# Products with the high and low halves side by side, and a moved gate conditioning, in a two-layer hybrid block

## The chip, the core and the metric

The kernel runs on one core of one Trainium2 chip, as one launch. The metric is the device time of an execution in microseconds (us), the median over runs. The profile is one execution, taken by the hardware profiler.

## What is computed

Two residual layers act on 256 latent tokens `x`, with 256 context tokens `ctx` beside them; the model width is 2048. Layer 0 is windowed attention with 16 heads and a sink, and it updates both token sets; layer 1 is latent attention (MLA), whose output is wanted for `x` alone.

```python
cond = silu(c); cond_ctx = silu(c_ctx)
for i in range(2):
    shift, scale, gate = split(cond @ ada_w[i] + ada_b[i], 3)     # and *_c from cond_ctx
    h  = rmsnorm(x, norm_g[i]) * (1 + scale) + shift
    hc = rmsnorm(ctx, norm_g[i]) * (1 + scale_c) + shift_c
    o, oc = swa_mixer(h, hc, ...) if i == 0 else mla_mixer(h, hc, ...)
    x = x + gate * o
    if i == 0: ctx = ctx + gate_c * oc
return x

def mixer(h, hc):                      # the outline of both
    q, k, v, g = split(h @ w_in)       # MLA: through two low-rank latents
    o = softmax(q @ k.T * scale + mask) @ v
    return (o * silu(g)) @ w_out
```

`gate` is the third section of the conditioning, `cond @ ada_w[i][:, 4096:]`; it is called the gate conditioning here, and `silu(g)` the output gate.

## The kernel before

**Precision.** Every float32 operand of a large product is split in two: `hi`, rounded to the format float32r, and `lo`, the rest (`split`: ScalarE copies, VectorE subtracts). `mm3` makes one product of three: high by high, high by low, low by high. Weights arrive as `raw` tiles by DMA and become `whi` and `wlo`; activations lie in `h` tiles.

**Stages.** Feature blocks of 128 (`kt`, 16 of them) are the contraction steps. Start: the 16 blocks of `xT` are loaded and squared, the sum of squares gives the norm's factor `rb`, and `ada_first_tasks(0)` makes the first shift and scale; `make_h0(kt)` then makes h. Stage A is the projection to q, k, v of all 512 tokens in five groups of blocks (1, 2, 3, 4 and 6 of them, `GROUPS`); beside a group run as `side` tasks the conditioning products of the next one. Stage B makes the output gates with the attention between. The first output projection (`out0_tasks`) follows: for blocks n below 9 (`XONLY`) first the 256 latent tokens, then blocks 9 to 15 for all 512 tokens at once, then the context half of blocks 0 to 8 (`late`). Layer 1 then has its low-rank projections, queries, keys and output gates (`gate_tasks` with n = 256, 17 of them, since the list holds head 14 twice) with attention between, and the last projection `out1_tasks`, 16 blocks.

In the 256-token products (output gates of layer 1, `out0` for one half, `out1`) the weights stand in the array and 256 tokens stream: three products of 256 columns for a contraction step.

**Gate conditioning.** VectorE makes it (`gate_half`): rows of `ada_w` come as `raw<-adag` tiles of 512 KB, 16 for each half of a layer's contraction, and every tile takes one `scalar_tensor_tensor` with a running sum for each 512 columns and token set. Layer 0's lies in stages A and B, layer 1's two halves (32 tiles) in the first output projection.

**Order.** The program is first noted as a list of operations (`Plan`). `settle` then gives each engine its order by due times (`clock`, `lead`), assumed costs (`cost`) and free buffers; the engines run that order as written. All loads go out of SyncE's (SP) queue, in one order, and `raw` has four buffers.

Of the kernel before, what the change touches and what calls it, by code (L numbers as in the profile page):

```python
# [29 lines left out]
POOL = 0.0  # L30
G0PREP, G0, G0B = 2, {4: (0, None)}, 0.7
# [3 lines left out]
SIDE = [0.85, 0.9, 0.8, 0.95, 1.0]  # L35
# [7 lines left out]
G1, G1CUT = 0.9, 29  # L43
# [93 lines left out]
class ToBe:  # L137


    def __init__(self, pool, shape, dt, tag, bufs, name, space):  # L140
        self.pool, self.shape, self.dt, self.tag = pool, shape, dt, tag
# [19 lines left out]
SWITCH, REACH, TURN, REACHT = 340.0, 20.0, 112.0, 0.0  # L161
DMA_LAT, DMA_RATE = 2000.0, 320.0


class Plan:
# [6 lines left out]
    def pool(self, real, bufs, space="SB"):  # L172
        plan = self

        class Pool:
            def tile(_, shape, dt, tag=None, name=None, bufs_=None, bufs=bufs):
                t = ToBe(real, list(shape), dt, tag, bufs, name, space)
# [126 lines left out]
    def settle(self):  # L304
# [37 lines left out]
        def give(tag):  # L342
            tiles = self.tags[tag]
            while head[tag] < len(tiles) and slots[tag]:
# [4 lines left out]
                s = min(slots[tag], key=lambda s: (s[2] not in (None, t.dt), s[0], s[1]))  # L349
                slots[tag].remove(s)  # L350
                t.slot, t.place = s[:2]
# [10 lines left out]
        while len(out) < len(nodes):  # L362
# [52 lines left out]
            for t in v.tiles:  # L415
                t.done = max(t.done, v.end if e != "PE" else at + v.occ + 120)
                left[id(t)] -= 1
                if not left[id(t)] and t.space != "DRAM":
                    tag = (t.space, t.tag)
                    slots[tag].append((t.done + SEM, t.place, t.dt))  # L420
# [3 lines left out]
    def emit(self):  # L424
# [3 lines left out]
        for v in order:  # L428
            for t in v.tiles:
                if t.real is None:  # L430
# [5 lines left out]
                    had = homes.get((tag, t.place))  # L436
                    if had is None or had[0] != t.dt:
                        had = homes[tag, t.place] = t.dt, t.pool.tile(
                            t.shape if own else [P, size[tag]], t.dt,
                            tag=f"{t.tag}_{t.place}", name=f"{t.name}_{t.place}", bufs=1)  # L440
                    x = had[1]
                    if not own:
                        x = x[:, :int(np.prod(t.shape[1:]))]
# [24 lines left out]
def tile_hybrid_two_layer(ctx: ExitStack, tc: tile.TileContext, a: dict):  # L468
# [4 lines left out]
    hp = plan.pool(ctx.enter_context(tc.tile_pool(name="hp", bufs=32)), 32)  # L473
# [33 lines left out]
    def htile(dt=F32R):  # L507
        return hp.tile([P, 512], dt, tag="h", name=nm("h"))
# [208 lines left out]
    ssq = tpps()  # L717

    def add_squares(sq, first, last):
        for t in range(4):  # L720
            mm(ssq[:, t:t + 1], sq[:, t * P:(t + 1) * P], ones[:, 0:1], first and t == 0, last and t == 3)
# [1165 lines left out]
```

## Time and profile before

| | |
|---|---|
| median of 3 runs | 1250.98 us (1250.64 to 1251.53) |
| profiled execution, its time | 1250.65 us |
| its span, first to last instruction | 1248.9 us |
| TensorE (PE) busy | 1227.3 us, 98% of the span |
| VectorE (DVE) busy | 920.0 us, 74% |
| ScalarE (ACT) busy | 595.8 us, 48% |
| moved by DMA | 249.87 MB, mean 200 GB/s |

The span is 1.75 us shorter than the profiled execution. A busy TensorE is not one at its peak: its matmuls overlap, so the distance between two starts, and not the length of a row, says what one costs.

### The profile page before, as it was taken

The numbers are of one execution on the slowest core, as the hardware profiler recorded it, in microseconds if no ns is written. First come the engines' busy times: TensorE is split into PE (matmuls) and PEld (weight loads), VectorE is DVE, ScalarE is ACT, GpSimd is POOL, SyncE is SP. The second block draws the span as 40 slices with busy tenths as digits, with TensorE's granted clock in tenths as the row PEclk, the third lists the DMA queues.
The fourth block names the chain that finished last, engine by engine and source line by source line (L and its number), as shares of the span: only waits on it lengthen the run. The fifth ranks groups of instructions, "written<-read, shape, count | busy, mean of one in ns | idle before, by whom it ended". The sixth has DMA issues, their size and how long they took to land.

```text
span 1248.9 us, 23671 instructions
## 1 busy us (share of the span) xinstructions
PE 1227.3 (98%) x8828; PEld 1075.7 (86%) x8828; DVE 920.0 (74%) x2255; ACT 595.8 (48%) x1434; POOL 79.1 (6%) x97
## 2 busy tenths in 40 slices
PE   6999999999999999999999999999999999999998
PEld 6788877888888888888899888899999999999998
DVE  3466636698569799977898766886778888878554
ACT  4613212322235445655764223454677777676332
POOL 0000000000001001101000000000111111110000
PEclk9999999999999999999999999999999999999999
DMA  9877677459885656755439967764433333322674
GB/s 324 288 266 251 209 242 240 130 188 334 270 295 199 229 172 230 263 189 180 138 117 289 324 232 246 258 219 118 136 127 111 110 110 110 99 97 85 212 225 138
DMA packets 105524, 249.87 MB, mean 200 GB/s; under 512 B 12352, under 2 KB 26176, under 8 KB 105408
## 3 DMA queue, kind: packets, MB, share of 16 engines
q1 hardware_dynamic: 105408, 248.36, 59.6%
q8 instruction: 69, 1.13, 0.4%
q14 instruction: 47, 0.39, 0.1%
HBM read 239.92 MB, written 8.39 MB: 199 GB/s over the span
## 4 chain that ended last, share of the span: by engine, by line
PE 94%; DVE 3%; DMA 2%; ACT 1%; issue 0%; SPq 0%; ACTq 0%; DVEq 0%
PE mm L236 79%; PE tp L236 8%; PE tp L221 4%; PE s L236 2%; PE s L221 1%; DVE wlo L221 1%; DVE t L221 1%; DMA raw<-adag 0%; DVE acc L221 0%; DMA raw<-wout 0%; DMA k<-ada 0%; DMA h<-xT 0%; ACT whi L221 0%; DVE h L221 0%; ACT t L221 0%
## 5 line engine op out<-in xcount | busy, mean ns | idle before, releaser
L236 PE MATMUL mm<-h,whi 128*128 128x256 f32 (+1 forms) x2368 | 537.4, 319 | 1.9 <-ACT whi L221 1.7
L221 ACT CAST whi<-raw 128x1024 fp32r<-128x1024 f32 (+3 forms) x248 | 243.7, 984 | 374.3 <-PE mm L236 301.8
L236 PEld LDWEIGHTS mm<-h,whi 128*128 128x128 f32 x2368 | 392.0, 191 | 29.3 <-ACT whi L221 2.5
L221 DVE TENSOR_TENSOR wlo<-raw,whi 128x1024 fp32r<-128x1024 f32 (+3 forms) x248 | 282.6, 1141 | 148.3 <-ACT whi L221 141.5
L236 PE MATMUL mm<-h,wlo 128*128 128x256 f32 (+1 forms) x1184 | 378.3, 320 | 3.8 <-DVE wlo L221 3.8
L236 PE MATMUL mm<-whi,h 128*128 128x512 f32 (+2 forms) x1152 | 358.3, 384 | 2.7 <-ACT h L221 2.0
L236 PEld LDWEIGHTS mm<-whi,h 128*128 128x128 f32 x1152 | 213.7, 188 | 44.2 <-issue 4.6
L236 PEld LDWEIGHTS mm<-h,wlo 128*128 128x128 f32 x1184 | 226.1, 191 | 20.2 <-DVE wlo L221 5.7
L236 PE MATMUL mm<-wlo,h 128*128 128x512 f32 (+2 forms) x576 | 220.6, 383 | 0.0
L236 PEld LDWEIGHTS mm<-wlo,h 128*128 128x128 f32 x576 | 108.3, 188 | 18.1 <-issue 0.4
L221 DVE SCALAR_TENSOR_TENSOR t<-raw,acc 128x512 f32<-128x512 f32 x128 | 85.8, 686 | 4.2 <-DMA raw<-adag 2.7
L221 DVE TENSOR_TENSOR acc<-acc,mm 128x512 f32<-128x512 f32 x96 | 63.7, 684 | 26.9 <-PE mm L236 26.6
L236 PE MATMUL mm<-pth,k 128*128 128x256 f32 x256 | 55.4, 289 | 0.0
L221 DVE TENSOR_REDUCE st<-tp 128x1 f32<-128x512 f32 (+1 forms) x76 | 45.9, 605 | 11.2 <-PE tp L236 10.8
L221 POOL TENSOR_TENSOR rr<-rr,mhalf 128x2 f32<-128x2 f32 (+2 forms) x41 | 29.7, 728 | 380.8 <-DVE rr L221 380.0
L236 PE MATMUL tp<-k,q 128*128 128x512 f32 (+1 forms) x189 | 46.4, 361 | 0.0
L221 ACT ACTIVATE cb<-tp,st,rq 128x512 f32<-128x512 f32 (+1 forms) x49 | 33.2, 677 | 27.3 <-DVE st L221 25.9
L221 POOL TENSOR_TENSOR rq<-rq,mhalf 128x2 f32<-128x2 f32 x32 | 27.3, 863 | 297.3 <-DVE rq L221 277.2
L221 POOL TENSOR_TENSOR rk<-rk,mhalf 128x4 f32<-128x4 f32 x20 | 21.9, 1093 | 377.2 <-DVE rk L221 373.8
L221 ACT ACTIVATE t<-acc 128x128 f32<-128x128 f32 (+2 forms) x70 | 26.6, 390 | 40.1 <-DVE acc L221 21.1
L221 ACT CAST pth<-tp 128x512 fp32r<-128x512 f32 x59 | 33.3, 586 | 23.9 <-PE tp L221 23.1
L236 PEld LDWEIGHTS mm<-pth,k 128*128 128x128 f32 x256 | 42.5, 190 | 1.0 <-issue 0.2
(186 smaller groups left out, 1466.5 us busy)
## 6 DMA issues: line engine op xcount, KB each, us to landing
k<-ada SPq DMA_DIRECT2D x128, 256.0 KB, 4.9
raw<-adag SPq DMA_DIRECT2D x64, 512.0 KB, 4.6
acc<-ada SPq DMA_DIRECT2D x128, 256.0 KB, 5.0
raw<-wout SPq DMA_DIRECT2D x47, 512.0 KB, 4.4
raw<-win SPq DMA_DIRECT2D x42, 512.0 KB, 4.6
raw<-mwg SPq DMA_DIRECT2D x34, 512.0 KB, 3.3
raw<-wgate SPq DMA_DIRECT2D x32, 512.0 KB, 5.8
raw<-mwo SPq DMA_DIRECT2D x29, 512.0 KB, 3.8
```

The source lines that it names most:

```text
L221: getattr(real, op)(*r, **k)
L236: getattr(real, op)(*[x.real() if isinstance(x, View) else x for x in args], **{n: x.real() if isinstance(x, View) else x for n, x in kw.i ...
```

## The change

1. **Side by side.** A pair of `h` tiles becomes one tile of 1024 columns (`hpair`). For each 256-token half it holds 256 high and 256 low columns next to each other, and `mmw` takes both in one product of 512 columns with the high weights; a second product of 256 columns adds low weights by high tokens to the first half of the result. The two halves of the result are added afterwards: in `gate_tasks` by an ACT copy and a DVE addition, in `fin_half` and `out1_tasks` by one more DVE operation. It is used for the layer-1 output gates, for `out0` where one half is made, and for `out1` except its last block. `out0` for both halves keeps three products of 512 columns, which now read two pieces of 256 (`both`).
2. **Gate conditioning.** Half of layer 1's (16 tiles) moves from the first output projection to groups 2 and 3 of stage A (`G1PREP`, `G10`).
3. **Start.** Squares are summed by DVE into two tiles instead of by TensorE for every pair of blocks; eight products `ones` by `xT` (`warm`, `WARM`) write a tile that nobody reads; `rms_bcast` works in pieces of 256 columns; `adab` and `normg` load later.
4. **Order.** `settle` lets SP run no further than `BACKLOG` ahead of the DMA it assumes, and hands out pairs of `h` places. This changes the order of loads all over the program.

```diff
-SIDE = [0.85, 0.9, 0.8, 0.95, 1.0]
+G1PREP, G10 = 2, {2: (0, 7), 3: (7, None)}
+WARM = range(6, 14)
+SIDE = [0.85, 0.9, 0.8, 0.9, 1.0]
-G1, G1CUT = 0.9, 29
+G1, G1CUT = 0.9, 17
+BACKLOG = 500.0
...
                 pipe[0] = begin + v.lat / DMA_RATE
                 v.end = pipe[0] + DMA_LAT
+                free[e] = max(free[e], pipe[0] - BACKLOG)
...
+    def hpair():
+        return hp.tile([P, 1024], F32R, tag="h", name=nm("h"), span=2)
...
+    def mmw(ps, lh, ll, pair, first, last):
+
+
+        mm(ps, lh, pair, first, False)
+        mm(ps[:, :256], ll, pair[:, :256], False, last)
...
-        sq = tmp()
-        S.activation(sq, t, AF.Square)
-        if kt % 2 and kt < KT - 1:
-            V.tensor_tensor(even, even, sq, op=ALU.add)
-            add_squares(even, kt == 1, False)
-        elif kt < KT - 2:
-            even = sq
+        if kt < 2:
+            S.activation(ssq[kt], t, AF.Square)
         else:
-            add_squares(sq, False, kt == KT - 1)
-    adab = const("adab", [P, 2, 48])
-    normg = const("normg", [P, 2, KT])
+            sq = tmp()
+            S.activation(sq, t, AF.Square)
+            V.tensor_tensor(ssq[kt % 2], ssq[kt % 2], sq, op=ALU.add)
+        if kt in WARM:
+
+            mm(warm, ones, t, True, True)
+            clock[0] = 0.0
+    with plan.lead(-4.0):
+        adab = const("adab", [P, 2, 48])
+        normg = const("normg", [P, 2, KT])
...
-                    hh, hl = h[kt] if n == NT else h1[0][kt]
-                    mm3(ps[:, :n], wh[:, us], wl[:, us], hh, hl, kt == 0, kt == KT - 1)
+                    if n == NT:
+                        mm3(ps, wh[:, us], wl[:, us], *h[kt], kt == 0, kt == KT - 1)
+                    else:
+                        mmw(ps, wh[:, us], wl[:, us], o0[kt][:, :512], kt == 0, kt == KT - 1)
...
+            if n == NX:
+                g = th[:, NX:]
+                S.copy(g, ps[:, NX:])
+                V.tensor_tensor(g, ps[:, :NX], g, op=ALU.add)
+                ps = g
...
+        if gi == G1PREP:
+            prep, g10 = gate_half(1, 1, 0, lambda i: gate0_tile(4 + i))
+            side = prep + side
+        if gi in G10:
+            s, e = G10[gi]
+            side = merge(side, g10[s:e]) if side else g10[s:e]
...
+    def both(kt):
+        t = o0[kt].rearrange("p (v i c) -> p v i c", v=2, i=2)
+        return t[:, :, 0, :], t[:, :, 1, :]
...
-                    oh, ol = o0[kt]
-                    mm3(box["ps"][:, vs], wh[:, us], wl[:, us], oh[:, vs], ol[:, vs],
-                        kt == 0, kt == KT - 1)
+                    if v0 < v1:
+                        mm3(box["ps"].rearrange("p (v c) -> p v c", v=2), wh[:, us], wl[:, us],
+                            *both(kt), kt == 0, kt == KT - 1)
+                    else:
+                        mmw(box["ps"], wh[:, us], wl[:, us], o0[kt][:, v0 * 512:(v0 + 1) * 512],
+                            kt == 0, kt == KT - 1)
...
+        if ps2 is not None:
+            V.scalar_tensor_tensor(x1[n][:, vs], ps2, ada[0][:, v, 32 + n:33 + n],
+                                   x1[n][:, vs], op0=ALU.mult, op1=ALU.add)
...
-                    mm3(box["ps"][:, :NX], wh[:, us], wl[:, us], *o1[kt], kt == 0, kt == KT - 1)
+                    if n < KT - 1:
+                        mmw(box["ps"], wh[:, us], wl[:, us], o1[kt], kt == 0, kt == KT - 1)
+                    else:
+                        mm3(box["ps"][:, :NX], wh[:, us], wl[:, us], *halves(o1[kt]), kt == 0,
+                            kt == KT - 1)
```

On TensorE's queue a block of the last projection (`out1_tasks`) stood before as three products for each of the 16 contraction steps (`h` the tokens' tile, `whi` and `wlo` the weights' halves):

```order
L236 MATMUL mm_0_311<-h_7_1804,whi_0_280 128x256
L236 MATMUL mm_0_311<-h_8_1825,wlo_0_289 128x256
L236 MATMUL mm_0_311<-h_10_1840,whi_0_280 128x256
L236 MATMUL mm_0_311<-h_9_1822,whi_0_280 128x256
L236 MATMUL mm_0_311<-h_10_1840,wlo_0_289 128x256
L236 MATMUL mm_0_311<-h_12_1993,whi_0_280 128x256
L236 MATMUL mm_0_311<-h_11_1983,whi_0_280 128x256
L236 MATMUL mm_0_311<-h_12_1993,wlo_0_289 128x256
L236 MATMUL mm_0_311<-h_14_2007,whi_0_280 128x256
L236 MATMUL mm_0_311<-h_13_2000,whi_0_280 128x256
```

and stands now as two, the first of 512 columns:

```order
L239 MATMUL mm_1_283<-h_4_1754,whi_0_236 128x512
L239 MATMUL mm_1_283<-h_4_1754,wlo_0_248 128x256
L239 MATMUL mm_1_283<-h_6_1772,whi_0_236 128x512
L239 MATMUL mm_1_283<-h_6_1772,wlo_0_248 128x256
L239 MATMUL mm_1_283<-h_8_1780,whi_0_236 128x512
L239 MATMUL mm_1_283<-h_8_1780,wlo_0_248 128x256
```

One of three products goes at every step, and the columns that stream stay 768. Over the program 1600 products of 256 columns with `whi` (two for a step) have become 800 of 512 columns, and TensorE's list is 819 rows shorter when rows that stand together are counted apart.

At the program's start TensorE's queue had, up to the first product of stage A (the sums of squares `ones` by `t`, the first conditioning `k` by `sil`, the factor's broadcast `t` by `ones`, and its transposes; of the nine sums the last):

```order
L236 MATMUL tp_0_174<-ones_81,t_3_172 128x1 x4
L236 MATMUL s_1_235<-k_0_127,sil_91 32x128 x4
L236 MATMUL s_1_235<-k_1_129,sil_91 32x128 x4
L236 MATMUL s_1_235<-k_2_131,sil_91 32x128 x4
L236 MATMUL s_1_235<-k_3_133,sil_91 32x128 x4
L236 MATMUL tp_2_258<-t_1_167,ones_81 128x512
L236 MATMUL s_1_235<-k_4_139,sil_91 32x128 x4
L236 MATMUL s_1_235<-k_5_141,sil_91 32x128 x4
L236 MATMUL s_1_235<-k_6_123,sil_91 32x128 x4
L236 MATMUL s_1_235<-k_7_125,sil_91 32x128 x4
L236 MATMUL tp_3_291<-ident_121,t_0_201 128x64 x2
L236 MATMUL mm_0_311<-whi_0_280,h_15_304 128x512
```

and has now, as far as the first conditioning product behind the broadcast:

```order
L239 MATMUL tp_0_127<-h_6_93,ones_81 128x512 x2
L239 MATMUL tp_0_127<-h_8_101,ones_81 128x512 x2
L239 MATMUL tp_0_127<-h_10_107,ones_81 128x512 x2
L239 MATMUL tp_0_127<-h_12_114,ones_81 128x512 x2
L239 MATMUL tp_1_179<-ones_81,q_0_109 128x1 x4
L239 MATMUL tp_1_179<-ones_81,q_1_96 128x1 x4
L239 MATMUL s_2_192<-k_0_152,sil_87 32x128 x4
L239 MATMUL s_2_192<-k_1_157,sil_87 32x128 x4
L239 MATMUL s_2_192<-k_2_168,sil_87 32x128 x4
L239 MATMUL s_2_192<-k_3_173,sil_87 32x128 x4
L239 MATMUL tp_3_221<-t_1_112,ones_81 128x256 x2
L239 MATMUL s_2_192<-k_4_177,sil_87 32x128 x4
```

The nine sums of four products each, spread over the loads, have become two at the end; the eight products `h` by `ones` stand ahead of them; the broadcast is two products of 256 columns.

On VectorE's queue, late in the first output projection (`raw` by `acc` is the gate conditioning of layer 1, `acc<-mm` the residual's addition, `h<-t` the norm of layer 1), ten rows before were:

```order
L221 SCALAR_TENSOR_TENSOR h_25_939<-t_1_167,ada_0_3363,h_26_951 128x256
L221 SCALAR_TENSOR_TENSOR t_2_169<-acc_7_378,ada_0_3363,q_2_7274 128x256
L221 SCALAR_TENSOR_TENSOR t_1_167,kn_1_2937<-raw_0_143,acc_13_442 128x512
L221 SCALAR_TENSOR_TENSOR acc_1_325<-mm_3_328,ada_0_297,t_3_172 128x256
L221 TENSOR_TENSOR wlo_0_289<-raw_1_145,whi_0_280 128x1024
L221 TENSOR_TENSOR acc_20_518<-acc_20_518,t_0_201 128x256
L221 SCALAR_TENSOR_TENSOR h_27_1155<-t_2_169,ada_0_3363,h_28_1167 128x256
L221 SCALAR_TENSOR_TENSOR t_3_172<-acc_2_331,ada_0_3363,q_2_7274 128x256
L221 TENSOR_TENSOR wlo_1_294<-raw_2_147,whi_1_287 128x1024
L221 SCALAR_TENSOR_TENSOR t_1_167,kn_1_2937<-raw_0_143,acc_6_361 128x512
```

and ten rows of the same place now are:

```order
L224 SCALAR_TENSOR_TENSOR t_3_119<-acc_5_350,ada_0_1927,q_0_7107 128x256
L224 TENSOR_TENSOR wlo_1_254<-raw_2_303,whi_1_250 128x1024
L224 SCALAR_TENSOR_TENSOR h_18_404<-t_1_112,ada_0_1927,h_18_404 128x256
L224 SCALAR_TENSOR_TENSOR acc_9_377<-mm_0_279,ada_0_259,t_2_99 128x256
L224 SCALAR_TENSOR_TENSOR h_20_537<-t_3_119,ada_0_1927,h_20_537 128x256
L224 SCALAR_TENSOR_TENSOR acc_9_377<-mm_0_279,ada_0_259,acc_9_377 128x256
L224 TENSOR_TENSOR wlo_0_248<-raw_1_208,whi_0_236 128x1024
L224 TENSOR_TENSOR acc_8_371<-acc_8_371,t_0_159 128x256
L224 SCALAR_TENSOR_TENSOR t_1_112<-acc_23_545,ada_0_1927,q_0_7107 128x256
L224 SCALAR_TENSOR_TENSOR t_0_159<-acc_1_295,ada_0_1927,q_0_7107 128x256
```

The two conditioning operations are gone from this stretch, and the residual's addition has become two operations. The last two conditioning operations still come some ten rows later.

## Rows read from the trace of the kernel before

**Rows 1.** Page, first part: busy us, share of the span, instructions.
```profile
PE 1227.3 (98%) x8828; PEld 1075.7 (86%) x8828; DVE 920.0 (74%) x2255; ACT 595.8 (48%) x1434; POOL 79.1 (6%) x97
```

**Rows 2.** Stretches of the span: busy time of each engine, clock, DMA.
```profile
core 0: us, PE busy (x) PEld busy (x) DVE busy (x) ACT busy (x) POOL busy (x), PEclk, DMA share, GB/s
0.00:31.60 31.60, 21.04 (x143) 18.81 (x143) 9.79 (x25) 13.00 (x23) 1.22 (x5) 1.00 0.98 325
...
100.00:155.00 55.00, 55.00 (x428) 44.55 (x427) 34.30 (x66) 15.29 (x23) 0.00 (x0) 1.00 0.65 221
155.00:225.00 70.00, 70.00 (x503) 53.88 (x503) 34.37 (x56) 14.02 (x19) 0.00 (x0) 1.00 0.69 233
225.00:318.00 93.00, 93.00 (x416) 76.89 (x415) 82.83 (x210) 25.94 (x52) 3.95 (x4) 1.00 0.67 228
...
650.00:820.00 170.00, 165.59 (x1054) 150.83 (x1053) 131.82 (x291) 67.23 (x106) 1.12 (x1) 0.99 0.79 263
...
870.00:1155.00 285.00, 283.19 (x1948) 264.92 (x1947) 229.29 (x596) 200.47 (x619) 42.87 (x52) 1.00 0.34 110
1155.00:1249.00 94.00, 89.10 (x731) 87.90 (x729) 46.82 (x57) 32.31 (x37) 0.00 (x0) 1.00 0.60 191
```

**Rows 3.** Waits of TensorE over the span: us in total, times, longest.
```profile
PE tp L236 <- DVE t L221: 8.6, 5, 7.4
PE mm L236 <- DVE wlo L221: 3.8, 5, 2.0
```

**Rows 4.** TensorE in time, stage A: start, length, operands, first and last.
```profile
94.65 0.39 PE L236 MATMUL mm<-wlo,h 128*128 128x512 f32 x1
...
103.49 0.39 PE L236 MATMUL mm<-wlo,h 128*128 128x512 f32 x1
```

**Rows 5.** The same, last projection: first and last of twelve rows.
```profile
1189.83 0.28 PE L236 MATMUL mm<-h,wlo 128*128 128x256 f32 x1
...
1193.79 0.28 PE L236 MATMUL mm<-h,wlo 128*128 128x256 f32 x1
```

**Rows 6.** Groups of instructions by shape: high weights by 256 tokens' columns.
```profile
L236 PE MATMUL mm<-h,whi 128*128 128x256 f32 x1632 | 304.2, 285 | 1.9 <-ACT whi L221 1.7 <-ACT h L221 0.2
```

**Rows 7.** Waits within 650 to 820 us, ScalarE's for the projection's weights.
```profile
ACT whi L221 <- DMA raw<-wout: 32.4, 10, 5.2
```

**Rows 8.** VectorE and TensorE in time at 799 us.
```profile
799.00 0.69 DVE L221 SCALAR_TENSOR_TENSOR t<-raw,acc 128x512 f32<-128x512 f32 x1 [2.15 <-DMA raw<-adag]
...
801.28 0.39 PE L236 MATMUL mm<-h,wlo 128*128 128x256 f32 x1 [2.04 <-DVE wlo L221]
```

**Rows 9.** One stretch behind that wait, columns as in Rows 2.
```profile
801.80:805.20 3.40, 3.40 (x18) 3.40 (x18) 3.40 (x8) 0.78 (x2) 0.00 (x0) 0.50 0.83 236
```

**Rows 10.** VectorE's groups by shape within 650 to 820 us.
```profile
L221 DVE SCALAR_TENSOR_TENSOR t<-raw,acc 128x512 f32<-128x512 f32 x64 | 42.4, 687 | 2.8 <-DMA raw<-adag 2.7
L221 DVE SCALAR_TENSOR_TENSOR acc<-mm,ada,t 128x256 f32<-128x256 f32 x30 | 13.9, 481 | 17.2 <-PE mm L236 16.9 <-DMA t<-xT 0.2
...
L221 DVE DVE_READ_ACCUMULATOR t<-raw,acc 128x1 f32 x64 | 5.3, 83 | 0.0
```

**Rows 11.** TensorE in time at the start, up to stage A's first product.
```profile
15.08 8.70 PE L236 MATMUL tp<-ones,t 128*128 128x1 f32 x40 [0.26 <-DVE t L221]
23.71 1.93 PE L236 MATMUL s<-k,sil 128*32 128x128 f32 x32
25.85 1.66 PE L236 MATMUL tp<-t,ones 128*128 128x512 f32 x2 [0.21 <-DVE t L221]
27.44 1.08 PE L236 MATMUL s<-k,sil 128*32 128x128 f32 x32
28.94 0.66 PE L236 MATMUL tp<-ident,t 128*128 128x64 f32 x4 [0.41 <-DVE t L221]
31.59 0.50 PE L236 MATMUL mm<-whi,h 128*128 128x512 f32 x1 [2.00 <-ACT h L221]
```

**Rows 12.** SP's queue in time: the last five loads of `xT`.
```profile
7.34 3.02 SPq L221 DMA_DIRECT2D h<-xT  x5
```

**Rows 13.** ScalarE and VectorE in time at the start: a square, a sum.
```profile
17.65 0.69 DVE L221 TENSOR_TENSOR t<-t,t 128x512 f32<-128x512 f32 x1 [0.92 <-ACT t L221]
...
18.70 0.63 ACT L221 ACTIVATE t<-q 128x512 f32<-128x512 f32 x1 [0.56 <-PE tp L236]
```

**Rows 14.** Page, DMA issues: KB each, us from issue to landing.
```profile
raw<-adag SPq DMA_DIRECT2D x64, 512.0 KB, 4.6
```

More of the change, by code (lines that the diff above doesn't have):

```diff
@@ L175, in pool, with tile @@
         class Pool:
-            def tile(_, shape, dt, tag=None, name=None, bufs_=None, bufs=bufs):
-                t = ToBe(real, list(shape), dt, tag, bufs, name, space)
+            def tile(_, shape, dt, tag=None, name=None, bufs_=None, bufs=bufs, span=0):
+                t = ToBe(real, list(shape), dt, tag, bufs, name, space, span)
                 plan.tags.setdefault((space, tag), []).append(t)
@@ L348, in give @@
                     continue
-                s = min(slots[tag], key=lambda s: (s[2] not in (None, t.dt), s[0], s[1]))
-                slots[tag].remove(s)
-                t.slot, t.place = s[:2]
+                if t.span == 2:
+                    by = {s[1]: s for s in slots[tag]}
+                    pairs = [(by[i], by[i + 1]) for i in by if i % 2 == 0 and i + 1 in by]
+                    if not pairs:
+                        head[tag] -= 1
+                        return
+                    s = min(pairs, key=lambda s: (any(x[2] not in (None, t.dt) for x in s),
+                                                  max(s[0][0], s[1][0]), s[0][1]))
+                    for x in s:
+                        slots[tag].remove(x)
+                    t.slot, t.place = max(s[0][0], s[1][0]), s[0][1]
+                else:
+                    s = min(slots[tag], key=lambda s: (s[2] not in (None, t.dt), s[0], s[1]))
+                    slots[tag].remove(s)
+                    t.slot, t.place = s[:2]
                 for v in parked.pop(id(t), ()):
@@ L419, in settle @@
                     tag = (t.space, t.tag)
-                    slots[tag].append((t.done + SEM, t.place, t.dt))
+                    for i in range(2 if t.span == 2 else 1):
+                        slots[tag].append((t.done + SEM, t.place + i, t.dt))
                     give(tag)
@@ L507, in htile @@
     def htile(dt=F32R):
-        return hp.tile([P, 512], dt, tag="h", name=nm("h"))
+        return hp.tile([P, 512], dt, tag="h", name=nm("h"), span=1)
+    def hpair():
+        return hp.tile([P, 1024], F32R, tag="h", name=nm("h"), span=2)
     def atile(dt=F32):
@@ L716, in tile_hybrid_two_layer @@
     xk = {}
[L717 to L721, printed above, removed]
+    ssq = [qtile(F32) for _ in range(2)]
+    warm = tpps()
     for kt in range(KT):
@@ L914, in rms_bcast @@
     def rms_bcast(sq, nt, then, wait=1.5):
-        tp = sq
-        if sq is not ssq:
-            tp = tpps()
+        tp = tpps()
+        for i, s in enumerate(sq):
             for t in range(nt):
-                mm(tp[:, t:t + 1], sq[:, t * P:(t + 1) * P], ones[:, 0:1], True, True)
+                mm(tp[:, t:t + 1], s[:, t * P:(t + 1) * P], ones[:, 0:1], i + t == 0,
+                   i + t == len(sq) + nt - 2)
         r = small(4, "rr")
@@ L1377, in tile_hybrid_two_layer @@
     g1 = []
-    for hf in range(2):
-        for t in gate_half(1, 1, hf, lambda i: atile()):
-            g1 += t
+    for t in gate_half(1, 1, 1, lambda i: atile()):
+        g1 += t
     queue.extend(merge(out0, g1[:G1CUT], G1))
@@ L1423, in tile_hybrid_two_layer, with halves @@
     lat = {}
-    halves = [o0[kt][i][:, NX:] for kt in range(KT) for i in range(2)]
-    halves_x = [o0[kt][i][:, :NX] for kt in range(KT) for i in range(2)]
+    pairs = [o0[kt][:, 512:] for kt in range(KT)]
+    pairs_x = [o0[kt][:, :512] for kt in range(KT)]
+    def halves(pair):
+        return pair[:, :256], pair[:, 256:]
     def mwy_piece(pr):
```

67 lines of the change are left out of this document (41 added, 26 removed).

## The prediction

> **What bounds the kernel now.** I read the busy times first. TensorE is busy for 98% of the span [rows 1], so only what shortens its queue, or the time in which it stands, can move the end. The list of its waits is short: 8.6 us for the sums of squares at the start and 3.8 us for low weights later [rows 3]. The table of stretches says where it stands: from 0 to 31.6 us (21.04 of 31.60 us busy, all of it preparation), and from 650 to 820 us, the first output projection (165.59 of 170). In stage A from 100 to 318 us it never stands, not even where VectorE is busy 82.83 of 93 us. From 870 to 1155 us it stands 1.81 us, and in the last 94 us 4.9 us, most of it the program's tail [rows 2].
>
> What a product costs is the distance between starts. In stage A thirteen triples of 512 columns lie between 94.65 and 103.49 us, 0.680 us each, so 0.2267 for one product [rows 4]. In the last projection eleven triples of 256 columns lie between 1189.83 and 1193.79 us, 0.360 each, so 0.120 for one [rows 5]. Twice the columns cost 1.89 times as much, not 2: each product carries some 0.013 us that doesn't grow with its columns.
>
> **Step 1, side by side.** A step of three products of 256 columns (0.360 us) becomes one of 512 and one of 256 (0.2267 + 0.120 = 0.3467). That saves 0.0133 us. The trace has 1632 products of the tokens with high weights at 256 columns [rows 6]; the changed order keeps 32 (the last block), so 1600 / 2 = 800 steps change: 288 in the first projection (9 blocks by 16 steps, for each token half), 272 in the 17 output gates, 240 in the last. 800 x 0.0133 = **10.7 us off**. No row shows 512 and 256 columns in turn. Bounds: nothing, if the wide product cost two narrow ones (0.240); and 16 us, if the pair cost its 768 columns at the wide price (0.340 us). I take 10.7, since both parts have a row at exactly their size.
>
> The Trainium skill, "TensorE: Matmul & The Clock Gate", section "Back-to-back issue gap", gives the spacing of warm products as their columns over 2.4 GHz plus about 2.5 ns. By it a removed product would save only those 2.5 ns, 2.0 us over 800 steps (an estimate from that page). The rows put 0.2267 us where that formula has 0.216, and 0.120 where it has 0.109; here I go by the rows.
>
> **Step 2, two pieces instead of one.** Where `out0` takes both halves at once (7 blocks, 16 steps, 3 products: 336), the moving side now reads two pieces of 256. No row shows it. Bounds: nothing, or one more product's fixed part, 336 x 0.0133 = 4.5 us. I take 0: the number of columns and of products is the same, and the fixed part is seen per product.
>
> **Step 3, additions of the halves.** VectorE and ScalarE do these beside TensorE. Per gate one copy and one addition, per block of a projection one operation like the 0.481 us one [rows 10]. In 870 to 1155 us VectorE has 229.29 of 285 us busy; 17 additions of at most 0.48 us make it 237.5, and the stretch gets 272 x 0.0133 = 3.6 us shorter: 84% busy instead of 80%. The cover is thin but was enough at 89% in stage A (82.83 of 93) [rows 2]. Further, the first product of a pair reads high and low together, so it waits for VectorE's low half where it used to start on ScalarE's high half; that counts only at the few places where TensorE stands for them, some 0.4 us each. I put **0.5 us on**; bounds 0 and 4 (the waits of 1.81 us in this stretch tripled).
>
> **Step 4, 16 tiles of gate conditioning leave 650 to 820 us.** TensorE stands 4.41 us there (170 - 165.59) [rows 2], and the granted clock is at 0.50, the lower of its two levels (1.2 GHz), for 3.4 us [rows 9], which costs another 1.7 us: 6.1 us in all. What precedes it is to be read at 799 us: VectorE stands 2.15 us in its order before a conditioning operation whose tile hasn't landed; the low weights queue behind it, and TensorE waits 2.04 us [rows 8]. ScalarE meanwhile waits 32.4 us for the projection's own weights [rows 7], so the loads are late in general. Half of the 64 operations of 0.687 us and of their 0.083 us reads go: 24.6 us of VectorE's 131.8; 18 operations of 0.481 us come, 8.7 us [rows 10]. Of the loads, 16 tiles of 512 KB are 8.4 MB out of 263 GB/s x 170 us = 44.7 MB, or 19% [rows 2, 14]. The order shows two operations left in the last part of this stretch, where the 2.04 us wait lay. I take **3.5 us off** of the 6.1; bounds: all 6.1, or 1 us on (the projection's own weights stay late, and TensorE asks for them 3.8 us sooner).
>
> **Step 5, the same tiles in stage A.** Groups 2 and 3 run from about 100 to 225 us, at 221 and 233 GB/s. 8.4 MB over 125 us add 67 GB/s, so some 295. At the start the queue moved 325 GB/s at a DMA share of 0.98. VectorE goes from 68.7 to 93.3 of 125 us; 32 tiles of the same kind in 225 to 318 us beside stage A stopped TensorE nowhere [rows 2]. The loads and not VectorE are what could run late. I put **1 us on**; bounds 0 and 7.5 (two waits like that of 799 us, 2.04 + 1.7 us each).
>
> **Step 6, the start.** Before, the sums of squares occupy TensorE to 15.08 + 8.70 = 23.78 us (40 records, 0.2175 us each), and stage A begins at 31.59, 7.8 us later. The conditioning products show the clock: 1.93 us at 23.71 against 1.08 at 27.44 for the same 32 records, so the lower level first, the upper (2.4 GHz) after [rows 11]; the clock column prints 1.00 for the whole start [rows 2], so I go by the durations. Now the blocks of `xT` land as before (the last is issued at about 10, and squares and sums of 0.63 and 0.69 us follow [rows 12, 13]), so VectorE's sums are ready near 18. TensorE first has eight products of 512 float32 columns. One took 1.66 us with the clock rising in it [rows 11]; at the upper level throughout I estimate half, 0.83. Eight take 6.6 to 13.3 us, and the queue's order lets them begin with the tenth load, near 10.7: they end between 17.3 and 24, I take 20.7. Then come 32 records of sums: 7.0 us at 0.2175, half, 3.5, at the upper level. 20.7 + 3.5 = 24.2, against 23.78. The chain behind is a little shorter, since the broadcast comes in pieces: 7.3 instead of 7.8. Stage A begins at 31.5: **0**. Bounds: 3 us sooner (18 + 3.5 + 7.3 = 28.8), or 7 us later (24 + 7.0 + 7.8 = 38.8, if the clock stays low).
>
> **Sum.** -10.7 - 3.5 + 0.5 + 1 + 0 = -12.7 us. Against the profiled execution's 1250.65 us this gives 1237.95, so 1238; that execution is 0.33 us below the median of the runs, which I leave in the rounding.
>
> **Rivals.**
> (a) *The products save as said, other waits take part of it back*: 1242 to 1248. The start with a clock that falls again (+4) or new waits in stage A (+3.7 each) are enough. For it: loads in groups 2 and 3 come near to what the queue has moved anywhere, and the whole order of loads is new. Against: no wait in stage A before.
> (b) *More than said*: 1228 to 1234. All 6.1 us of step 4 return, and the start gains 3: 1238 - 2.6 - 3 = 1232.4, and less still if steps 3 and 5 cost nothing.
> (c) *A wide product costs what two narrow ones do*, so step 1 gives nothing: 1250.65 - 3.5 + 1.5 = 1248.7, within 0.2%. For it: no row with both shapes in turn. Against: [rows 4, 5]. The page named in step 1 points this way; by its gap, 1250.65 - 2.0 - 2.0 = 1246.7 (an estimate).
> (d) *Slower: stage A's tiles block VectorE.* The mechanism of 799 us [rows 8, 9] moves along: VectorE stands before a conditioning operation of group 2 or 3, the low weights come late, TensorE stands 2.04 us, and the clock falls for 1.7 more. At 3.7 us each, five of the 16 tiles cost 18.5 us against 13.7 gained without step 5's 1 us: 1250.65 - 13.7 + 18.5 = 1255.5. It decides from four tiles on (14.8). Against: 32 tiles passed in 225 to 318 us with TensorE standing nowhere.
>
> **How the numbers follow.** A measurement of this kernel tells about 0.2%, 2.5 us, from no change. Forecast (1234 to 1242, likeliest 1238): 0.52. (a) 0.19. (b) 0.17. (c) 0.05. (d) 0.07. Faster holds the first three, 0.88; same is (c), 0.05; slower is (d), 0.07. The range leaves out the far half of (b), the last part of (a), and (c) and (d): 1232 to 1246.
>
> **What would show it.** Right: in the last projection a step of one 512 and one 256 column product every 0.347 us; 650 to 820 us without the half clock, and with TensorE's idle time under 2 us; 100 to 225 us still full. Wrong in step 1: 0.36 us a step. Wrong in step 6: stage A's first product later than 34 us, or long conditioning products ahead of it. Wrong in step 5: waits for low weights, or VectorE waiting for `raw<-adag`, between 100 and 225 us. What would break the forecast most is a price of the wide product that differs among narrow ones, since five sixths of the gain are that one number times 800.

## The result, and the profile after

The changed kernel takes **1237.27 us** (median of 4, 1234.63 to 1238.83) where the kernel before takes 1251.26 beside it: a ratio of 0.9881, 95% interval 0.9869 to 0.9894, 1.2% faster. Measured again later it gave 0.9877 (0.9862 to 0.9892). The forecast was 1238 (1232 to 1246). The profiled execution took 1236.39 us with a span of 1234.6, 14.24 us shorter than before's, where the sum said 12.7. The total was right; several terms of the sum were not, and their errors cancelled in part, which is luck.

First the busy times, as [rows 1]:

```profile
PE 1211.6 (98%) x7990; PEld 1020.5 (83%) x7990; DVE 944.0 (76%) x2313; ACT 598.9 (49%) x1452; POOL 80.3 (7%) x97
```

TensorE has 838 matmuls fewer (800 of them in the changed steps) and 15.7 us less of busy time; VectorE has 24 us more. The table of stretches, columns as in [rows 2]:

```profile
0.00:31.60 31.60, 17.28 (x131) 10.91 (x132) 15.00 (x33) 14.91 (x27) 1.22 (x5) 1.00 0.89 306
...
100.00:155.00 55.00, 55.00 (x459) 42.73 (x452) 41.75 (x92) 14.02 (x22) 0.00 (x0) 1.00 0.91 317
155.00:225.00 70.00, 68.88 (x462) 53.62 (x461) 45.07 (x98) 15.76 (x21) 0.00 (x0) 1.00 0.76 270
225.00:318.00 93.00, 93.00 (x415) 76.92 (x414) 83.21 (x210) 25.77 (x55) 4.66 (x5) 1.00 0.70 232
...
650.00:820.00 170.00, 169.03 (x869) 143.57 (x868) 125.38 (x251) 71.76 (x111) 0.70 (x1) 1.00 0.68 226
...
870.00:1155.00 285.00, 282.03 (x1649) 247.65 (x1647) 239.61 (x622) 205.40 (x635) 43.64 (x51) 1.00 0.35 111
1155.00:1235.00 80.00, 76.28 (x439) 66.70 (x439) 44.80 (x55) 26.25 (x25) 0.00 (x0) 0.97 0.65 200
```

From 650 to 820 us TensorE now stands 0.97 us (4.41 before) and the clock is whole. The loads there fell from 263 to 226 GB/s and rose from 221 to 317 in 100 to 155 us, where TensorE still never stands; from 155 to 225 us it now stands 1.12 us. From 870 to 1155 us it stands 2.97 us and not 1.81, and behind 1155 the clock reads 0.97. TensorE's waits, as [rows 3]:

```profile
PE tp L239 <- DVE q L224: 11.4, 1, 11.4
PE mm L239 <- DVE h L224: 1.6, 2, 0.9
PE mm L239 <- DVE wlo L224: 1.5, 3, 0.8
PE s L239 <- DMA k<-ada: 1.1, 2, 0.9
```

The waits for low weights went from 3.8 to 1.5 us; those for the low halves of tokens (`h`) went from 0.7 us (one wait) to 1.6 (two), and two for conditioning weights (`k<-ada`) are new.

To place the 14.24 us, and to compare the experiments, the span is cut at five events that every kernel has: stage A's first product, the last store of `spill`, the last reload of `kn`, the first product with `mwx` and the last with the second query weights. Each figure is the time in us from one event to the next, from the starts in one trace. The rows below "changed" are kernels of the experiments that follow.

| kernel | start | A | B | first projection | gates, attention | last projection, tail | span |
|---|---|---|---|---|---|---|---|
| before | 31.59 | 300.85 | 260.84 | 259.59 | 258.92 | 137.06 | 1248.85 |
| changed | 29.02 | 299.95 | 261.91 | 250.79 | 256.59 | 136.35 | 1234.61 |
| changed, again | 30.14 | 303.36 | 262.78 | 251.69 | 256.49 | 134.22 | 1238.68 |
| three narrow | 29.22 | 300.20 | 262.51 | 254.72 | 258.64 | 136.66 | 1241.95 |
| half moved back | 29.55 | 299.87 | 263.32 | 262.02 | 256.67 | 134.21 | 1245.64 |
| queue unbounded | 29.72 | 308.61 | 261.30 | 250.37 | 256.91 | 134.68 | 1241.59 |
| eight and eight | 30.26 | 301.45 | 262.48 | 252.92 | 253.49 | 134.98 | 1235.58 |

Two traces of the same kernel differ by up to 3.4 us in stage A and 2.1 us in the last projection, so a single row resolves no less than that; whole times are compared by ratios over the runs.

### The profile page after: what moved, and what is told of

It is laid out like the page before. It is cut to its first block, busy times and chain, and to the rows that moved or that the text cites. A ratio compares the mean times of both kernels' runs of the same rounds, so it can differ in the third digit from the quotient of the medians.

```text
span 1234.6 us, 22038 instructions
## 1 busy us (share of the span) xinstructions
PE 1211.6 (98%) x7990; PEld 1020.5 (83%) x7990; DVE 944.0 (76%) x2313; ACT 598.9 (49%) x1452; POOL 80.3 (7%) x97
## 4 chain that ended last, share of the span: by engine, by line
PE 93%; DVE 3%; DMA 2%; ACT 1%; issue 1%; SPq 0%; POOL 0%; DVEq 0%; ACTq 0%
PE mm L239 78%; PE tp L239 7%; PE tp L224 4%; PE s L239 4%; PE s L224 1%; DVE t L224 1%; DVE wlo L224 1%; DMA acc<-crow 1%; SPq L224 0%; DMA h<-xT 0%; DMA raw<-adag 0%; DVE acc L224 0%; DMA k<-ada 0%; ACT t L224 0%; POOL rr L224 0%
## 5 line engine op out<-in xcount | busy, mean ns | idle before, releaser
L239 PE MATMUL mm<-h,whi 128*128 128x512 f32 (+1 forms) x1568 | 527.6, 396 | 1.6 <-DVE h L224 0.9
L224 DVE TENSOR_TENSOR wlo<-raw,whi 128x1024 fp32r<-128x1024 f32 (+3 forms) x248 | 282.4, 1140 | 111.3 <-ACT whi L224 109.1
L239 PEld LDWEIGHTS mm<-h,whi 128*128 128x128 f32 x1568 | 290.4, 188 | 61.2 <-ACT whi L224 1.7
L224 DVE SCALAR_TENSOR_TENSOR t<-raw,cb 128x512 f32<-128x512 f32 x96 | 62.6, 687 | 13.1 <-DMA raw<-adag 12.9
L224 DVE SCALAR_TENSOR_TENSOR t<-raw,acc 128x512 f32<-128x512 f32 x96 | 64.9, 686 | 4.2 <-DMA raw<-adag 2.4
L224 DVE TENSOR_REDUCE st<-tp 128x1 f32<-128x512 f32 (+1 forms) x66 | 39.2, 594 | 10.2 <-PE tp L239 9.6
L224 DVE TENSOR_TENSOR ptl<-tp,pth 128x512 fp32r<-128x512 f32 x61 | 41.0, 686 | 3.6 <-ACT pth L224 3.2
```

The source lines that it names most:

```text
L224: getattr(real, op)(*r, **k)
L239: getattr(real, op)(*[x.real() if isinstance(x, View) else x for x in args], **{n: x.real() if isinstance(x, View) else x for n, x in kw.i ...
```

## The experiments

Each kernel ran five times or so beside the kernel before. One thousandth of a ratio is 1.25 us; a difference between two ratios is uncertain by some 2 us.

**1. The changed kernel again.** No edit.

> The changed kernel itself once more, beside the three below on one chip. All theories: 1236 to 1239, ratio 0.987 to 0.990. Its trace says what varies from one execution to the next: if the lower clock at the start of the last projection (1154.69 to 1158.10 us in its first profile) belongs to the stalls before it, it is there again; if it comes in some executions only, it may be gone with the same stalls of 0.945 and 0.444 us.

Measured: 1237.52 us, ratio 0.9877 (0.9862 to 0.9892). The stalls at the start of the last projection were there again (0.950 and 0.454 us), without the lower clock. So that clock (below) belongs to some executions, not to the stalls alone. What had not been expected is the price of a step. Here is TensorE in time in the last projection, in the changed kernel's first profile:

```profile
1190.03 0.40 PE L239 MATMUL mm<-h,whi 128*128 128x512 f32 x1
...
1191.09 0.40 PE L239 MATMUL mm<-h,whi 128*128 128x512 f32 x1
```

And in this one:

```profile
1189.92 0.39 PE L239 MATMUL mm<-h,whi 128*128 128x512 f32 x1
...
1190.96 0.40 PE L239 MATMUL mm<-h,whi 128*128 128x512 f32 x1
```

Three steps, each a wide and a narrow product, lie between the two rows each time: 1.06 us in the first, 1.04 in the second. The stream repeats one of two patterns, often for a hundred steps and more: 0.3533 us a step, or 0.3467, the value of the prediction. A small delay of one product can change it from one to the other, as in the first profile at 794 us:

```profile
791.14 0.40 PE L239 MATMUL mm<-h,whi 128*128 128x512 f32 x1
...
792.20 0.40 PE L239 MATMUL mm<-h,whi 128*128 128x512 f32 x1
...
794.20 0.31 PE L239 MATMUL mm<-h,wlo 128*128 128x256 f32 x1
794.35 0.40 PE L239 MATMUL mm<-h,whi 128*128 128x512 f32 x1
...
795.05 0.39 PE L239 MATMUL mm<-h,whi 128*128 128x512 f32 x1
...
796.09 0.39 PE L239 MATMUL mm<-h,whi 128*128 128x512 f32 x1
```

Ahead of the delay (a narrow product takes 0.15 us from start to start, not 0.117) three steps take 1.06 us, behind it 1.04. But it needs no delay. In the second trace the stream goes from the faster pattern to the slower one, in the middle of a block, with no product late by more than 0.01 us:

```profile
792.65 0.39 PE L239 MATMUL mm<-h,whi 128*128 128x512 f32 x1
...
793.69 0.39 PE L239 MATMUL mm<-h,whi 128*128 128x512 f32 x1
...
794.73 0.40 PE L239 MATMUL mm<-h,whi 128*128 128x512 f32 x1
...
795.79 0.40 PE L239 MATMUL mm<-h,whi 128*128 128x512 f32 x1
```

The traces of experiments 5 and 6 do the same at 797 and 793 us. Of the nine traces in which the last projection runs wide and narrow in turn, five have 0.3467 there and four 0.3533.

**2. Step 1 undone.**

```
-        mm(ps, lh, pair, first, False)
-        mm(ps[:, :256], ll, pair[:, :256], False, last)
+        mm3(ps[:, :256], lh, ll, pair[:, :256], pair[:, 256:], first, last)
```
The additions of the halves go too.

> The changed kernel with step 1 alone undone: each wide and narrow pair is three products of 256 columns again, and the additions of the halves are gone. Theory T (the product term was mis-sized: in the changed kernel a wide product takes 0.230 to 0.236 us and a narrow one 0.117 in turn, so a step takes 0.350 to 0.353 and not 0.3467): 800 steps give back 0.007 to 0.0095 us each, 5.6 to 7.6 us, less up to 1 us of stalls in the last projection that go with the additions, so 1242 to 1245, and a step of 0.360 in the last projection. Rival R (the term was 10.7 us as predicted, and waits elsewhere took part of it back): 1247 to 1249.

Measured: 1243.78 us, ratio 0.9931 (0.9918 to 0.9943), 5.0 to 5.4 thousandths above the changed kernel: 6.3 to 6.8 us. The last projection's step is 0.360 again. Theory T holds, R falls.

**3. The conditioning's half moved back** to the first projection (`G1PREP` and `G10` gone, both halves in `g1`, `G1CUT` 29).

> The changed kernel with layer 1's first half of the gate conditioning moved back from stage A to the first output projection. Theory T (the move is worth the 5 us by which TensorE's stands and the half clock in 650 to 820 us went away): 1241 to 1244, and TensorE stands over 3 us again between 650 and 820 us, with a stretch at the lower clock. Rival R (the stands went because of the shorter products and the other order of loads, not because of the move): 1236 to 1238.5, with TensorE's idle time there still under 2 us.

Measured: 1246.63 us, ratio 0.9948 (0.9934 to 0.9962): 8.4 to 8.9 us, more than T said. It lies in the first projection, 262.02 us where the changed kernel takes 250.79 and the kernel before 259.59. The stretch:

```profile
650.00:820.00 170.00, 163.51 (x820) 134.95 (x819) 135.55 (x299) 66.85 (x103) 1.13 (x1) 1.00 0.77 259
```

One of ScalarE's waits in it (us in total, times, longest):

```profile
ACT whi L224 <- DMA raw<-wout: 48.9, 21, 5.8
```

And TensorE's:

```profile
PE mm L239 <- DVE wlo L224: 6.1, 11, 0.8
```

TensorE stands 6.49 us, in many short waits, and the clock stays whole (T expected it to fall). ScalarE waits 21 times for the projection's own weights. Its waits in the same stretch of the changed kernel:

```profile
ACT whi L224 <- PE mm L239: 62.5, 27, 4.4
...
ACT whi L224 <- DMA raw<-wout: 4.2, 1, 4.2
```

There it waits once for them, and otherwise for TensorE to give weight buffers back: the loads are ahead.

**4. Which resource the moved half took.** The kernel of experiment 3, once with short operations and once with short loads for that half (its result is left out in both):

```
+                        c = 8 if (layer, hf) == (1, 0) else 512
-                        V.scalar_tensor_tensor(jk, w[:, q * 512:(q + 1) * 512], 0.5, box["cb"][2 * v + q],
+                        V.scalar_tensor_tensor(jk[:, :c], w[:, q * 512:q * 512 + c], 0.5,
+                                               box["cb"][2 * v + q][:, :c],
...
-            dict(src=a["adag"][layer, n, hf], n=1024, gen=gen(n), split=False, key=None)
+            dict(src=a["adag"][layer, n, hf][:, :nc], n=nc, gen=gen(n), split=False, key=None)
```

> The kernel with the conditioning's half moved back (8.4 us slower than the changed one by the ratios, with 14 waits of TensorE for low weights, 7.2 us), but the 32 operations of the half that was moved read 8 columns in place of 512; all its tiles are still loaded. The result of this half is left out. Theory V (the waits come from VectorE's time: 32 operations of 0.687 us stand ahead of the low weights, and VectorE is busy 135.55 of 170 us): TensorE's waits for low weights under 3 us, and 1239 to 1242. Theory D (the loads come late: 8.4 MB more between 650 and 820 us, at a DMA share of 0.77): the waits stay above 5 us, and 1245 to 1247.

> The same kernel the other way round: the 32 operations run at full size, on a tile that is there already, and the 16 loads of this half are 8 columns in place of 1024. The result of this half is left out. Theory V: the waits stay above 5 us, and 1245 to 1247. Theory D: the waits fall under 3 us, and 1239 to 1242. If both this and the one with short operations fall, VectorE waits for the tiles in its order, and each half of the mechanism is needed.

Measured: ratio 0.9956 (0.9944 to 0.9968) with short operations, 0.9943 (0.9928 to 0.9958) with short loads; the waits of TensorE stayed in both. The stretch with short operations:

```profile
650.00:820.00 170.00, 163.73 (x825) 135.92 (x824) 120.30 (x302) 66.78 (x103) 1.13 (x1) 1.00 0.78 260
```

TensorE's waits in it:

```profile
PE mm L239 <- DVE wlo L224: 5.6, 9, 1.2
```

The stretch with short loads:

```profile
650.00:820.00 170.00, 163.75 (x828) 136.64 (x827) 138.16 (x305) 67.28 (x104) 1.13 (x1) 1.00 0.66 213
```

TensorE's waits in it:

```profile
PE mm L239 <- DVE wlo L224: 6.0, 10, 1.1
```

Both theories fall in the form they were given: neither 15 us of VectorE's time nor 46 GB/s of traffic, taken away alone, frees the stretch. A kernel without both was not run, and the planner gives each of these kernels an order of its own, so that either alone is enough to slow the stretch is not ruled out. What both kernels keep is the place of 16 more tiles in the one order of loads, and the four `raw` buffers which these tiles share with the weights. SP's list points there: from 650 to 820 us it waits 26.0 us (36 times) for VectorE's operations that write `t`, nearly all of them conditioning operations that give a `raw` tile back, in experiment 3, and 9.0 us (19) in the changed kernel. Whether it is the buffers or the order of issue was not tried; that part stays argued.

**5. The other order of loads taken back.**

```
-BACKLOG = 500.0
+BACKLOG = 1e9
```

> The changed kernel with the planner's queue limit taken away, so that SP's loads stand in the order of before's rule. The prediction gave this part no term of its own. Theory T (the order of loads matters only together with the moved conditioning, and the queue has room): within 2 us of the changed kernel on the same chip, 1236 to 1240. Rival R (the limit is what keeps low weights from coming late while the conditioning tiles load): TensorE waits over 3 us more for low weights between 100 and 225 or between 650 and 820 us, and the time is 3 to 8 us up.

Measured: 1243.28 us, ratio 0.9928 (0.9914 to 0.9941), 5.1 thousandths or 6.4 us above the changed kernel on the same chip. Neither theory had the place right: the loss is in stage A, 308.61 us against 299.95 to 303.4 in the changed kernel's two traces. TensorE's waits from 31 to 230 us:

```profile
PE s L239 <- DMA k<-ada: 2.3, 2, 2.0
PE mm L239 <- ACT h L224: 1.4, 1, 1.4
```

From 215 to 225 us the clock reads 0.88, where both traces of the changed kernel have 1.00. These waits and the clock are part of the loss; where the rest of the 6.4 us lies is not shown. The first projection is unharmed (250.37).

**6. No long products at the start** (`WARM` empty).

> The changed kernel without the eight long products at the start. VectorE's last sum of squares ends at 18.5 us and the long products at 20.0, so the sums can begin 1.5 us sooner, but without them the clock is low. Theory T (the long products pay for themselves: sums at the lower level take 3.7 us and not 1.84, and the conditioning products behind them 1.93 and not 1.08): stage A's first product near 30 us and not 29.0, and the time 0.5 to 2 us up, 1238 to 1239.5. Rival R (the 2.6 us at the start come from the sums on VectorE, and the long products only delay): first product near 28, the time 1 us down, 1236.

Measured: 1238.46 us, ratio 0.9894 (0.9876 to 0.9913). TensorE in time without them:

```profile
18.52 3.57 PE L239 MATMUL tp<-ones,q 128*128 128x1 f32 x16 [18.52 <-DVE q L224]
22.02 1.93 PE L239 MATMUL s<-k,sil 128*32 128x128 f32 x32
```

And with them, in the changed kernel:

```profile
11.42 8.70 PE L239 MATMUL tp<-h,ones 128*128 128x512 f32 x16 [11.42 <-DVE q L224]
19.96 1.84 PE L239 MATMUL tp<-ones,q 128*128 128x1 f32 x16
21.73 1.08 PE L239 MATMUL s<-k,sil 128*32 128x128 f32 x32
...
29.02 0.50 PE L239 MATMUL mm<-whi,h 128*128 128x512 f32 x1 [1.06 <-ACT h L224]
```

The durations are as T said: double, at the lower level (1.2 GHz). But the sums end at 22.0 against 21.7 us, and stage A's first product (30.26) lies within the scatter of the kernels with them (29.02 to 30.83). The time is 1.3 to 1.7 thousandths up, within the uncertainty: not told apart. The traces also show that the long products do not keep the clock up. In eleven of the thirteen traces of the changed kernel and its variants, with the long products or without, it reads 0.50 for 3.4 us as stage A begins; only the changed kernel's first profile and experiment 2's are spared, and so is the kernel before. In the changed kernel's second trace:

```profile
30.55:33.97 3.42, 3.42 (x10) 2.68 (x9) 0.45 (x2) 1.17 (x2) 0.00 (x0) 0.50 0.98 362
```

That costs half of the stretch, 1.7 us, and is about half of the 3.4 us by which the two traces differ in stage A.

**7. Wide and narrow products in runs of two.** The narrow product is held back until two wide ones have gone.

```
         mm(ps, lh, pair, first, False)
-        mm(ps[:, :256], ll, pair[:, :256], False, last)
+        held.append((ps[:, :256], ll, pair[:, :256], last))
+        if len(held) == TURNS:
+            for p_, l_, r_, z_ in held:
+                mm(p_, l_, r_, False, z_)
+            held.clear()
```

> The changed kernel with the side by side products in the order wide, wide, narrow, narrow, over two steps of the contraction, in the gates and both projections; nothing else changes. Theory T1 (going between 512 and 256 columns costs the 0.003 to 0.007 us by which a step exceeds 0.3467): half of the changes go, so 0.5 x 800 x 0.005 = 2 us off, 1235, and two steps in the last projection take about 0.700 us where they take 0.707. Theory T2 (a wide product whose moving side is high and low halves is slow by itself): no change, 1236.5 to 1238, and 0.707.

Measured: 1237.54 us, ratio 0.9882 (0.9864 to 0.9899): no change. The stores of blocks 4 and 14 of the last projection are 55.73 us apart, 160 steps of 0.3483 us, which looked like T1 until experiment 1 showed 0.3467 without it. And where the first projection got ahead, it stood longer at the last heads' low halves:

```profile
655.21 0.73 PE L240 MATMUL mm<-h,whi 128*128 128x512 f32 x2 [2.15 <-DVE h L225]
```

**8. Runs of eight, and with four early blocks** (`TURNS` 8, ending with a piece of weights; `EARLY1` 4).

> The changed kernel with the side by side products in runs of eight wide and eight narrow ones (a run ends with its piece of weights; the last step of a block stays wide, narrow). In turn a step took 0.3534 us in the last projection, two and two 0.3483. Theory T1 (the excess over 0.3467 belongs to the changes of width): an eighth of the changes is left, so 0.3475 or less a step, and 800 x 0.005 = 4 us off the changed kernel on the same chip, of which one to two may go again at the waits for the last attention heads: 1233 to 1236. Theory T2 (what two and two gained comes from something else, as the pairing of weight loads): no further gain over 0.3483, and the whole time as that of the changed kernel.

> The kernel of eight and eight with four blocks of the last projection begun ahead of the last heads' results and not three. Theory T (the stalls of 0.945 and 0.444 us at the start of the last projection come because the work that covers the last heads' chain ran out sooner): some 4 us more of cover, the two stalls gone or under 0.5 us in sum, 1 us off the kernel with three, and up to 1.7 more in executions in which the clock fell there. Rival R (they wait for weights whose buffers come free late, which a fourth block makes worse): the stalls stay or grow, and the time is the same or 1 us up.

Measured: 1236.77 us, ratio 0.9874 (0.9860 to 0.9887), and 1235.87 us, 0.9872 (0.9858 to 0.9886): as the changed kernel. The last projection's steps take 0.351 us in both, so T1 falls for good: fewer changes of width don't shorten a step. That a wide product is slow by itself (T2 of experiment 7) falls with experiment 1. The part with the gates is some 3 us shorter (253.49 and 253.84), and 1.2 to 3.0 us of that go again in the first projection, where TensorE stands 2.37 us at 653 us for the last heads. The fourth early block left 1.3 us of stalls at the last projection, by other waits, where three had left 1.5: no gain.

**9. High halves first** in the last four steps of the early blocks, with three and with four early blocks.

```
+    def mmh(ps, lh, ll, pair, last):
+        mm(ps[:, :256], lh, pair[:, :256], False, False)
+        mm(ps[:, :256], ll, pair[:, :256], False, False)
+        mm(ps[:, :256], lh, pair[:, 256:], False, last)
```

> The changed kernel, but the last four steps of the three blocks that each projection begins early are three products of 256 columns with the high half first, so that they can start before VectorE's low half is there. Theory T (step 3's wait for the low half): at the start of the last projection the stall of 0.945 us (product at 1152.62, ScalarE's high half at 1152.1, VectorE's low half at 1152.57) falls to about 0.5, that at 652 us stays at 0.8, since there low weights wait behind VectorE's added operation; 24 steps cost 0.01 us more each, so the time is the same within 1 us, 1236 to 1239. Rival R (the stalls belong to the chain as a whole): no stall changes.

> The same with four early blocks in the last projection, in which the kernel of eight and eight lost the stall of 1.30 us. Theory T (what is left there is cover): the stalls at the start of the last projection are under 0.8 us in sum, 1235 to 1238, 0.5 to 1.5 us below the changed kernel in the same place of the trace, from the last product of the queries' projection to the last block. Rival R (weights' buffers): stalls as before, 1237 to 1239.

Measured: 1240.17 us, ratio 0.9892 (0.9870 to 0.9914), and 1240.29, 0.9891 (0.9877 to 0.9905): not better than the changed kernel, so none of these kernels beats it beyond doubt. The wait for the low half is gone, as T said, and another stands in its place; TensorE from 1140 to 1165 us with three blocks:

```profile
PE mm L239 <- ACT whi L224: 1.2, 2, 0.6
PE mm L239 <- ACT h L224: 0.2, 1, 0.2
```

The two stalls make 0.636 + 0.565 us in place of 0.945 + 0.444. With four blocks TensorE stands 1.8 us there, not under 0.8 as T said.

## Why the prediction was right, step by step

The mechanism was right in the main: the wide products, the conditioning moved away and the earlier start each shortened the stage they were meant for. The sizes were not: step 1 was 3 to 4 us too large, steps 4 and 6 together 3 to 5 us too small, and that these cancel is luck.

**Step 1 was too large.** The term put 800 steps at 0.0133 us, 10.7 us. Undisturbed steps (wide to next wide) average 0.3497 us in the first projection, 0.3518 in the gates and 0.3532 in the last; the three narrow products they replace averaged 0.3594, 0.3592 and 0.3599. So 288 x 0.0097 + 272 x 0.0074 + 240 x 0.0067 = 6.4 us; the second trace, with the faster pattern in the last projection, gives 7.8, and undoing the step, additions included, cost 6.3 to 6.8. Pricing each shape from its own uniform stream gave the faster of two patterns, and the mix is in it only part of the time. Rival (c), no gain, falls. So does the estimate of 2.0 us that the prediction worked out from 2.5 ns for a removed product in the Trainium skill, "TensorE: Matmul & The Clock Gate", section "Back-to-back issue gap"; that section gives the formula for an isolated product, and no price for a mix of widths.

**Step 2 was right.** Products that read two pieces of 256 take 0.227 us, as those of one piece. Between these rows of the changed kernel's first profile lie eight triples, 0.680 us each:

```profile
739.82 0.61 PE L239 MATMUL mm<-h,whi 128*128 128x512 f32 x2
...
745.26 0.61 PE L239 MATMUL mm<-h,whi 128*128 128x512 f32 x2
```

**Step 3 was about right in its waits, and left out what the clock can make of them.** VectorE's added operation does stand ahead of low weights at 652 us, as the trace in time shows:

```profile
652.08 0.48 DVE L224 SCALAR_TENSOR_TENSOR acc<-mm,ada,acc 128x256 f32<-128x256 f32 x1
...
652.48 0.48 DVE L224 SCALAR_TENSOR_TENSOR acc<-mm,ada,t 128x256 f32<-128x256 f32 x1
...
652.88 0.68 DVE L224 TENSOR_TENSOR wlo<-raw,whi 128x512 fp32r<-128x512 f32 x1
...
653.62 0.39 PE L239 MATMUL mm<-h,wlo 128*128 128x256 f32 x1 [0.80 <-DVE wlo L224]
```

Little of this 0.80 us is new, though: the kernel before stands 0.57 us for low weights near the same place, at 657.57 us. At the start of the last projection it stood three times:

```profile
1166.31 0.85 PE L236 MATMUL mm<-h,whi 128*128 128x256 f32 x3 [0.24 <-ACT h L221]
...
1167.91 0.50 PE L236 MATMUL mm<-h,whi 128*128 128x256 f32 x2 [0.40 <-ACT whi L221]
1168.85 0.39 PE L236 MATMUL mm<-h,whi 128*128 128x256 f32 x1 [0.45 <-ACT whi L221]
```

Now the wait for the low half has come there (0.94 us), with more behind it in the first profile:

```profile
1151.40:1154.69 3.29, 1.76 (x7) 0.79 (x5) 2.11 (x6) 1.94 (x3) 0.00 (x0) 1.00 0.01 4
1154.69:1158.10 3.41, 3.32 (x10) 2.85 (x11) 2.34 (x4) 0.61 (x2) 0.00 (x0) 0.50 0.75 232
```

TensorE stands 1.53 of 3.29 us where it stood 1.09 before, some 0.5 us more, which is what the prediction had for all of step 3. Then it runs 3.4 us at 0.50 of its clock (1.2 GHz), which costs 1.7 and had no term; it came in this execution and not in six others with the same stalls. It is part of why 1.6 us of shorter steps in the last projection show as 0.71; in the second trace, without the fall, the stage is 2.84 us shorter.

**Step 4 was too small, and it was not a term by itself.** The forecast was 3.5 of 6.1 us. The first projection got 8.80 us shorter, 2.8 of them by step 1, so 6.0, near the term's far bound. Four kernels of the table show more: from before's 259.59 us (that kernel has the old start and order of loads too) the move without side by side (three narrow) gives 4.9; side by side without the move (half moved back) takes 2.4 **longer**; both together give 8.8. This fits a stretch in which the loads set the pace and shorter products only turn into waits; apart from the new order of loads it was not tested. The sum of the prediction added the two as if they were independent. Of its mechanism, neither VectorE's time nor the amount loaded showed by itself in experiment 4; that the weights' loads come late was right.

**Step 5 was about right, with the queue limit.** Stage A takes 301.6 us on average over the nine traces with the half in it and the limit, 299.7 over the three with the half moved back: 1.9 us where the forecast said 1. (Two of the nine lack the clock fall of experiment 6; the other seven make 302.0, so 2.3.) VectorE does wait for the moved tiles between 100 and 230 us (11.5 us, 5 times), which the prediction named as a sign against step 5, but TensorE hardly. The 32 tiles which the prediction set against rival (d) were 16: in the kernel before, VectorE has 61 of these operations from 225 to 318 us, four to a tile. Without the limit stage A takes 308.61, 9 us more: a loss where rival (d) looked for one, but by other waits and a clock fall, not by its mechanism. The prediction had no term for the other order of loads, yet step 5's +1 rests on it.

**Step 6 was wrong by a count.** The sums of squares are 16 records and not 32, so 1.84 us and not 3.5 at the upper level; with the long products ending at 19.96 instead of 20.7 the sums end at 21.73 and not 24.2, and stage A began 0.8 to 2.6 us sooner, at best (29.02) near the early bound of 28.8. The clock fall of experiment 6, which only rival (a) had thought of, takes up to 1.7 of this back.

Stage B got 0.5 to 2.8 us longer in every kernel of the change, and only the one without the queue limit is near the kernel before (261.30). Nothing here settles that.

## What to carry to other kernels

Price a mix of shapes from the mix, or take a range between its parts and half the gain: a uniform stream shows the best case only. Ask of each saving on the bounding engine whether its operands keep up there; if loads set the pace, price it together with the change to the loads, for here the move alone went with 4.9 us, the shorter products alone with -2.4, and both with 8.8. And when tiles move into a stretch with a DMA share of 0.9, the order of issue is a term of its own, here 6.4 us.

## What the runs showed of the hardware

A stream of 512 and 256 columns in turn has two rhythms, 1.04 and 1.06 us for three steps. It went from one to the other at a delay of 0.03 to 0.08 us in one product, and in three traces with none over 0.01; what sets the choice stays open. In the last projection the slower one came behind a clock fall in the first profile and in the first kernel of experiment 9, and without one in the kernel with short operations and the second of experiment 9. Equal stalls of 0.95 and 0.45 us were followed by the lower clock in the first profile and not in six others of the same order; stalls of 0.64 and 0.57 us were followed by it in the first kernel of experiment 9. And while the sums of squares ran the clock column reads 1.00 both without the long products, where they took 3.57 us, and with them, where they took 1.84: at the start durations, not the column, tell the level.
